# Group A's attention: keys on the partitions, 512 queries in a row, and maxima from products of their own

## The chip, the cores and the metric

One Trainium2 chip; the kernel runs on one of its cores. The engines named below are PE (matrix products; PEld is its weight load), DVE (vector), ACT (scalar, which also evaluates the exponential), POOL (GpSimd) and SP, whose queue issues most of the transfers. The metric is the time of one execution on the device in microseconds (us); the median of three runs is given.

## The reference

The program is one step of a trunk layer with D = 1024 for 2048 latent tokens and 256 context tokens. A combined projection feeds three head groups: A, attention with 6 query heads and 2 key heads of 64; B, a gated DeltaNet in two directions; C, neighbourhood attention. Their outputs are joined by an output projection, and a SwiGLU follows. The change is in group A, where every latent query attends to all 2048 latent and 256 cached keys; context queries attend to the 256 context keys:

```python
def one_block(q_blk):
    sc = jnp.einsum('bqhgd,bkhd->bhgqk', q_blk, k).astype(jnp.float32) * scale
    p = jax.nn.softmax(sc, axis=-1).astype(v.dtype)
    return jnp.einsum('bhgqk,bkhd->bqhgd', p, v)
...
o_a = blocked_attention(qa, jnp.concatenate([ka, ka_ctx.astype(dt)], axis=1),
                        jnp.concatenate([va, va_ctx.astype(dt)], axis=1))
```

Group B solves a small triangular system per chunk of 64 tokens and then runs over the chunks in order (v_new = u - w s; s = s decay + k v_new), both ways.

## The kernel before

Tokens lie in tiles of 128: 16 latent, 2 context, so 18 key tiles with the cached ones. The stages run one after the other: phase_b projects group B, phase_ac projects C and then A and meanwhile prepares the DeltaNet, group_a is the attention, group_c and phase_out follow, then the ffn.

Operands of attention are split into a high and a low part (each exact in the fast product type). KA holds the keys transposed: partitions 0 to 63 the high parts, 64 to 127 the low parts of the same 64 dimensions, for both key heads. k_split makes it: PE transposes a tile of keys in which each dimension stands twice, ACT copies all 128 partitions as the high part, and DVE subtracts that from the second half (split_stack). q_stack does likewise for a tile of 128 queries and gives the high and low part of q, both on all 128 partitions.

group_a before goes through pairs of query tiles (index g, 8 latent and 1 context) and pairs of heads (pr); within these through 2 heads and 2 tiles, which gives 96 latent passes of 128 queries and one head. A pass has

- the scores with queries on the partitions: per 512 keys two products (high q, low q) against KA, in three PSUM tiles Sa and Sb (1024 keys) and Sc (256);
- on DVE the maximum of each (line 1220) and of the three (1224); on ACT the exponentials into P with the maximum as bias and the row sums as a by-product (1228);
- 18 transposes of P by PE (function turn) and their copies into PT by ACT (evac, line 1034), since the product with V needs the keys on the partitions;
- after four passes, the product with V (pv_pieces): 64 columns of weights, 256 queries, both heads into the halves of one PSUM tile po; later a transpose of the result and a multiplication by the reciprocal row sums, and a transfer to oa_d.

turn's and pv_pieces' pieces wait in lists (trs, pvs, late, extra) and are taken out one at a time between the score products, so that PE has work while DVE and ACT are at the maxima and exponentials. The order in which the code is written is the order of PE's instructions; on the others a scheduler places what is written, and what stands under high_priority comes earlier.

Two things run beside the attention. From pass RA = 6 on each pass takes one step of recur, the recurrence over the chunks (PSUM tile rx, tiles rS, rv, rU; its Pool operation rSe; line 971). And bg.run(2.0) lets the solves of the triangular systems go on (lines 843 and 844: a product into stmp and a reduction into sW), up to an estimate of that many us.

The start of A hangs on phase_ac's end: the last k_split writes KA (lines 1022, 1023), v_load brings V, and the first two query tiles have been stacked.

Of the kernel before, what the change touches and what calls it, by code (L numbers as in the profile page):

```python
# [18 lines left out]
NLAT = 16  # L19
NCTX = 2  # L20
NT = 18
# [38 lines left out]
class K:  # L60
# [34 lines left out]
    def setup(self):  # L95
        nc, a = self.nc, self.a
        self.ident = self.ctile("ident", [128, 128])
        nc.sync.dma_start(self.ident, a["ident"])
        self.mhalf = self.ctile("mhalf", [128, 1])
        nc.gpsimd.memset(self.mhalf, -0.5)  # L100

# [290 lines left out]
    def phase_ac(self, es_a, es_p, HB=3):  # L392
# [6 lines left out]
        self.qp = [es_p.enter_context(tc.tile_pool(name="A_q", bufs=2))]  # L399
        self.Q, self.qds = {}, {}  # L400
        es3 = ExitStack()
        bps = es3.enter_context(tc.tile_pool(name="b_ps", bufs=2, space=PSUM))
        with ExitStack() as es:
# [172 lines left out]
            kds = {}  # L576

# [14 lines left out]
            def k_dups(q):  # L592
                KS, KSp = self.KA
                kd = kds.pop(q)
                if q < 4:
                    self.k_split(KS, kd, [(i % 2, 4 * q + i // 2) for i in range(8)], bps)
                elif q == 4:
                    self.k_split(KSp, kd[:, 4:8], [(i % 2, i // 2) for i in range(4)], bps)
                else:
                    self.k_split(KS, kd[:, 0:4], [(i % 2, NLAT + i // 2) for i in range(4)], bps)  # L600

            def after(t):
# [5 lines left out]
                if t in (4, 5):  # L608
                    self.q_load(t - 4, kdp, 2)
                if t in (10, 11):  # L610
                    self.q_stack(t - 10, 0, 4, bps)
                    self.q_stack(t - 10, 4, 6, bps)
# [12 lines left out]
            with tc.high_priority(offset=HP):  # L625
                while pend:
                    a_flush()
            self.need_solves(0)
# [225 lines left out]
    def recur(self, wk, bank):  # L854
# [88 lines left out]
        for n in range(36):  # L943
# [40 lines left out]
            for d in range(2):  # L984
                v.tensor_copy(vn[hf[d], d], pv[hf[d], :256])
# [19 lines left out]
            v.tensor_copy(o, po)  # L1005
# [13 lines left out]
    def split_stack(self, dst, p):  # L1019
# [3 lines left out]
        nc.vector.tensor_tensor(dst[64:128], p[64:128], dst[64:128].bitcast(F32), ALU.subtract)  # L1023
# [22 lines left out]
    def k_split(self, KS, src, dst, pst):  # L1046
# [4 lines left out]
        for i0 in range(0, n, 4):  # L1051
# [5 lines left out]
            for i in range(m):  # L1057
# [6 lines left out]
                self.split_stack(KS[:, h, 128 * j:128 * (j + e - i)], p[:, 128 * i:128 * e])  # L1064

    def q_stack(self, t, h0, h1, pst):

        if h0 == 0:
            self.Q[t] = [self.qp[t // 2 % 2].tile([128, 6, 128], F32R, tag=f"q{n}", name="q", bufs=2) for n in "hl"]
        self.q_split(self.Q[t][0][:, h0:h1], self.Q[t][1][:, h0:h1], self.qds[t][:, h0:h1], h1 - h0, pst)  # L1070

# [16 lines left out]

    def group_a(self):
        nc, tc, a = self.nc, self.tc, self.a  # L1090
        self.EV = ()
        self.oa_d = [self.dtile(f"oa{t}", [128, 384]) for t in range(NT)]
        with ExitStack() as es:
            sp = es.enter_context(tc.tile_pool(name="A_p", bufs=2))
            tp = es.enter_context(tc.tile_pool(name="A_pt", bufs=4))
            wk = es.enter_context(tc.tile_pool(name="A_w", bufs=2))
            self.qp.append(wk)
            psS = es.enter_context(tc.tile_pool(name="A_S", bufs=1, space=PSUM))
            pst = es.enter_context(tc.tile_pool(name="A_t", bufs=2, space=PSUM))
            pso = es.enter_context(tc.tile_pool(name="A_o", bufs=1, space=PSUM))  # L1100
            rec = self.rec = self.recur(self.rwk, lambda: pst.tile([128, 512], F32, tag="pt", name="rx"))
            KS, KSp = self.KA
            V, Vp = self.VA
            groups = [(2 * g, 2 * g + 1) for g in range(NT // 2)]
            OA = {}
            Q = self.Q
            q_load = lambda t: self.q_load(t, wk, 1)
            q_stack = lambda t, h0, h1: self.q_stack(t, h0, h1, pst)

            def pv_pieces(g, pr, PT, rs):  # L1110

                lat = g < 8
                nk = NT if lat else 2
                Vx = V if lat else Vp
                st = {}

                def mm(j0, j1):
                    if j0 == 0:
                        st["po"] = pso.tile([128, 256], F32, tag="po", name="po")
                    for j in range(j0, j1):  # L1120
                        for h2 in range(2):
                            self.pe.matmul(st["po"][64 * h2:64 * h2 + 64, :], lhsT=Vx[:, j, (2 * pr + h2) // 3, :],
# [912 lines left out]
```

## Time and profile before

| | |
|---|---|
| median of 3 runs | 3837.43 us (3836.22 to 3840.2) |
| the profiled execution's own time | 3837.47 us |
| its span in the trace | 3835.5 us |
| granted PE clock, mean | 0.974 |
| first score product of group A to the last latent product with V | 826.7 to 1625 us |

The profile is of one execution. Its page gives busy shares of the engines and 40 slices of the span (95.9 us each); group A's latent part lies in slices 9 to 17:

```profile
PE   8997999969999999989999969999999998899999
PEld 5887988956777777778878869999999998688787
DVE  4784477689655555568765576677667664322433
ACT  4223322236666666657865643343334333322221
POOL 0002322620000000000003355556555553000111
```

Each digit is the busy share in tenths. A group's row reads: line, engine, operation, output <- inputs, shapes, count, then busy us and the mean of one in ns, then how long the engine stood idle ahead of it and for what. A row of the timeline has start, duration and operation. Matrix products overlap their neighbours, so their durations add up to more than the time that they take.

### The profile page before, as it was taken

What the parts mean: (1) busy time and instruction counts of PE and PEld (TensorE: products, weight loads), DVE (VectorE), ACT (ScalarE), POOL (GpSimd) and SP (SyncE); (2) the same over time, 40 slices, a digit from 0 to 9 for tenths busy, and PEclk for the clock granted to TensorE, in tenths of its full rate; (3) what the DMA queues carried; (4) which work ended last, traced back from release to release, by engine and by line L of the source; (5) the groups of instructions that cost most, each with busy time, mean ns of one, the idle gap of its engine ahead of it and who ended that gap; (6) DMA issues with size and microseconds to landing.
All of it is one profiled execution on the core that took longest, in us unless ns stands there. A gap on an engine that the chain in (4) does not pass through costs nothing. (4 is left out here: it accounts for less than half of the span.)

```text
span 3835.5 us, 64839 instructions
## 1 busy us (share of the span) xinstructions
PE 3607.6 (94%) x24526; PEld 3166.5 (83%) x24526; DVE 2308.8 (60%) x4786; ACT 1723.1 (45%) x3552; POOL 966.3 (25%) x1135
## 2 busy tenths in 40 slices
PE   8997999969999999989999969999999998899999
PEld 5887988956777777778878869999999998688787
DVE  4784477689655555568765576677667664322433
ACT  4223322236666666657865643343334333322221
POOL 0002322620000000000003355556555553000111
PEclk9998999989999999999999989999999999899999
DMA  7565877741211112255325643333333332633654
GB/s 270 200 210 175 259 223 225 197 116 48 55 48 51 44 46 52 64 160 144 90 79 186 213 132 99 98 108 108 105 93 97 101 96 75 208 111 125 194 187 133
DMA packets 649081, 501.15 MB, mean 131 GB/s; under 512 B 253681, under 2 KB 577120, under 8 KB 646464
## 3 DMA queue, kind: packets, MB, share of 16 engines
q1 hardware_dynamic: 645984, 493.41, 42.9%
q8 instruction: 193, 3.16, 0.4%
q10 hardware_dynamic: 2624, 3.55, 0.3%
q14 instruction: 120, 0.98, 0.1%
q0 software_dynamic: 160, 0.05, 0.0%
HBM read 348.14 MB, written 148.73 MB: 130 GB/s over the span
## 5 line engine op out<-in xcount | busy, mean ns | idle before, releaser
L37 PE MATMUL pd<-wd,ao 128*128 128x512 f32 x2376 | 550.3, 394 | 26.1 <-DMA wr<-in_w_down_dram 15.0
L37 PEld LDWEIGHTS pd<-wd,ao 128*128 128x128 f32 x2376 | 450.6, 190 | 125.7 <-ACT ao L1695 15.4
L37 PE MATMUL Y<-hop,gop 128*128 128x384 f32 x2376 | 452.3, 338 | 22.4 <-ACT hop L1695 9.8
L1034 ACT ACTIVATE PT<-pt 128x512 f32<-128x512 f32 (+1 forms) x600 | 331.9, 553 | 256.3 <-PE pt L37 249.4
L37 PEld LDWEIGHTS Y<-hop,gop 128*128 128x128 f32 x2376 | 422.1, 191 | 24.2 <-ACT hop L1695 10.1
L1696 DVE TENSOR_TENSOR gop<-S,gop 128x512 fp32r<-128x512 f32 x264 | 235.6, 893 | 167.3 <-ACT gop L1695 157.6
L37 PE MATMUL X<-hop,gop 128*128 128x384 f32 x1584 | 306.2, 342 | 18.7 <-DVE hop L1696 8.9
L37 PE MATMUL po<-PT,V 128*64 128x256 f32 (+1 forms) x3072 | 313.5, 341 | 2.2 <-ACT PT L1034 1.9
L37 PE MATMUL pso<-whi,hi 128*128 128x384 f32 (+2 forms) x864 | 288.8, 334 | 25.3 <-ACT whi L255 13.8
L37 PEld LDWEIGHTS X<-hop,gop 128*128 128x128 f32 x1584 | 283.5, 190 | 20.8 <-DVE hop L1696 9.6
L37 PE MATMUL pt<-ident,P 128*128 128x128 f32 x1752 | 284.9, 280 | 14.9 <-ACT PT L1034 7.9
L37 PE MATMUL Z<-hop,gop 128*128 128x384 f32 x1584 | 297.7, 336 | 0.0
L37 PE MATMUL pso<-whi,lo 128*128 128x384 f32 (+2 forms) x864 | 282.6, 327 | 7.6 <-DMA lo<-hl 7.6
L37 PE MATMUL pso<-wlo,hi 128*128 128x384 f32 (+2 forms) x864 | 282.9, 327 | 0.8 <-DVE wlo L256 0.5
L37 PEld LDWEIGHTS Z<-hop,gop 128*128 128x128 f32 x1584 | 278.7, 189 | 0.1
L37 PEld LDWEIGHTS pt<-ident,P 128*128 128x128 f32 x1752 | 200.3, 141 | 94.4 <-ACT PT L1034 36.3
L1695 ACT ACTIVATE gop<-S 128x512 fp32r<-128x512 f32 x264 | 166.2, 630 | 228.2 <-PE Y L37 124.9
L971 POOL TENSOR_TENSOR rSe<-rS,eh 64x128 f32<-64x128 f32 x144 | 55.0, 400 | 811.6 <-DVE rS L1003 780.9
L1696 DVE TENSOR_TENSOR gop<-wr,gop 128x512 fp32r<-128x512 f32 x198 | 200.9, 1015 | 83.8 <-ACT gop L1695 77.6
L37 PEld LDWEIGHTS po<-PT,V 128*64 128x64 f32 x3072 | 180.4, 136 | 79.3 <-issue 33.7
L1695 ACT ACTIVATE gop<-wr 128x512 fp32r<-128x512 f32 x198 | 125.2, 632 | 245.3 <-PE Z L37 174.7
L1696 DVE TENSOR_TENSOR ao<-ar,ao 128x1408 fp32r<-128x1408 f32 x72 | 127.4, 1769 | 145.1 <-ACT ao L1695 143.1
(323 smaller groups left out, 7208.1 us busy)
## 6 DMA issues: line engine op xcount, KB each, us to landing
ar<-a SPq DMA_DIRECT2D x72, 704.0 KB, 4.8
wr<-in_w_gu_dram SPq DMA_DIRECT2D x66, 512.0 KB, 4.1
wr<-in_w_gu_dram SPq DMA_DIRECT2D x132, 256.0 KB, 3.4
a<-o SPq DMA_DIRECT2D x396, 64.0 KB, 2.1
wm<-in_w_mod_dram SPq DMA_DIRECT2D x48, 512.0 KB, 4.1
hi<-hh SPq DMA_DIRECT2D x36, 512.0 KB, 5.4
lo<-hl SPq DMA_DIRECT2D x36, 512.0 KB, 6.4
st<-ptk SPq DMA_DIRECT2D x18, 768.0 KB, 4.1
```

The costliest lines, as they stand in the source:

```text
L37: r = f(*x, **kw)
L971: nc.gpsimd.tensor_tensor(Se[hh[x], d], S[hh[x], d, :, hh[x]], e.unsqueeze(2).to_broadcast([64, 2, 64]), ALU.mult)
L1034: self.nc.scalar.activation(out, p, AF.Copy)
L1695: self.nc.scalar.activation(hi, raw, AF.Copy)
L1696: self.nc.vector.tensor_tensor(lo, raw, hi.bitcast(F32), ALU.subtract)
```

## The change

Group A goes through 15 units instead: 4 latent blocks of 512 queries and the context block of 256, each with 3 pairs of heads (p with p + 3, so one head of either key head). Per unit and key tile j:

- scores with the keys on the partitions: for each of the two heads two products of 512 queries into one PSUM tile ST: KA against the high part of q (QH), and K1 against QL. K1 holds the keys' high part on 64 partitions and a row of ones as the 65th; QL holds the low part of q and, in its 65th row, minus the query's maximum. So ACT takes the exponential without a bias.
- P then already has the keys on the partitions, so the product with V uses it as it is (512 queries per product); the transposes of P and their copies are gone.
- the row sums, now sums over partitions, are collected: Pool adds most P tiles up (accp), DVE every sixth (accd); at the unit's end a product with ones sums over the partitions, and transposes bring sums and output to queries on the partitions.
- the maxima come from products of their own, of high parts alone, with queries on the partitions (SM; max_steps): 40 per unit (4 query tiles, 2 heads, 5 pieces of up to 512 keys), each reduced by DVE. They are made during the unit before. Four small products turn the maxima of one head into a row, which ACT copies into QL.

The first unit's maxima are written into the last sweep of the projections (mid) and, for the last piece of the latent keys, to the start of A. There too K1 is filled: a copy of KA's high half per key head from SBUF to SBUF by SP's queue and a fill with ones by DVE. For that, k_split puts the high part of key head 1 on partitions 64 to 127 (flip). The queries of the first block are loaded and stacked ahead of A, four tiles instead of two. In recur two copies out of PSUM move from DVE to ACT; the transfer of the output moves from ACT's queue to SP's. bg.run gets 0.9 per key tile and recur 0.45 of a step.

The core of the diff:

```diff
+            psM = es.enter_context(tc.tile_pool(name="A_M0", bufs=2, space=PSUM))
+            self.mg0 = self.max_steps(0, 0, self.mx0, psM, (4, 0, 1, 2))
...
             def mid(t0, j, i):
                 if t0 == NT - HB:
                     with tc.high_priority(offset=HP):
                         for f, q in MID.get((j, i), ()):
                             f(q)
+                        for _ in range(4):
+                            next(self.mg0, None)
...
-                v.tensor_copy(vn[hf[d], d], pv[hf[d], :256])
+                nc.scalar.activation(vn[hf[d], d], pv[hf[d], :256], AF.Copy)
...
-            v.tensor_copy(o, po)
+            nc.scalar.activation(o, po, AF.Copy)
...
+    def max_steps(self, b, p, mx, psM, chunks):
+        ks, nk, nq = (self.KA[0], 2304, 512) if b < 4 else (self.KA[1], 256, 256)
+        for c in chunks:
+            w = min(512, nk - 512 * c)
+            for qi in range(nq // 128):
+                for x in range(2):
+                    S = psM.tile([128, 512], F32, tag="SM", name="SM")
+                    self.pe.matmul(S[:, :w], lhsT=self.QB[b][0][:, p + 3 * x, 128 * qi:128 * qi + 128],
+                                   rhs=ks[:, x, 512 * c:512 * c + w], start=True, stop=True)
+                    with self.tc.high_priority(offset=1000):
+                        self.nc.vector.tensor_reduce(mx[:, qi, x, c:c + 1], S[:, :w], AX.X, ALU.max)
+                    yield
...
+            for x, y in zip(self.K1, self.KA):
+                nc.vector.tensor_copy(x[64:65].rearrange("p h k -> p (h k)"),
+                                      self.one[64:65, 0:1].to_broadcast([1, 2 * x.shape[2]]))
+                for h in range(2):
+                    nc.sync.dma_start(x[0:64, h].bitcast(F32), y[64 * h:64 * h + 64, h].bitcast(F32))
+            psS = es.enter_context(tc.tile_pool(name="A_S", bufs=3, space=PSUM))
+            psM = es.enter_context(tc.tile_pool(name="A_M", bufs=2, space=PSUM))
+            pso = es.enter_context(tc.tile_pool(name="A_o", bufs=1, space=PSUM))
...
+            def maxes(b, p, at=None):
...
+                yield from self.max_steps(b, p, mx, psM, (3,) if at else range(nch))
...
+                with tc.high_priority(offset=1000):
+                    nc.vector.tensor_reduce(mn[:, :n], mx[:, :n, :, :nch], AX.X, ALU.max, negate=True)
+                QL = self.QB[b][1]
+                for x in range(2):
+                    t = pst.tile([128, 512], F32, tag="pt", name="mrow")
+                    for qi in range(n):
+                        self.pe.matmul(t[64:65, 128 * qi:128 * qi + 128], lhsT=mn[:, qi, x:x + 1], rhs=self.ident,
+                                       start=True, stop=True, skip_group_check=True)
+                    with tc.high_priority(offset=1000):
+                        nc.scalar.activation(QL[64:65, p + 3 * x, :nq], t[64:65, :nq], AF.Copy)
+                    yield
...
+            def scores(b, p, j):
...
+                P = sp.tile([128, 2, 512], F32, tag="P", name="P")
...
+                for x in range(2):
+                    S = psS.tile([128, 512], F32, tag="S", name="ST")
...
+                    self.pe.matmul(S[:, :nq], lhsT=ks[:, x, kc], rhs=QH[:, h, :nq], start=True, stop=False)
+                    self.pe.matmul(S[:, :nq], lhsT=k1[0:65, x, kc], rhs=QL[0:65, h, :nq], start=False, stop=True)
+                    nc.scalar.activation(P[:, x, :nq], S[:, :nq], AF.Exp)
+                return P
...
+                for x in range(2):
+                    self.pe.matmul(po[64 * x:64 * x + 64, :nq], lhsT=V[:, j, x, :], rhs=P[:, x, :nq], start=(j == 0),
+                                   stop=(j == nk - 1), skip_group_check=True)
+                if j % 2 == 0:
+                    next(mg, None)
...
+                if j % 6 == 5:
+                    ad = accs[1][:, :, :nq]
+                    if j == 5:
+                        nc.vector.tensor_copy(ad, w)
+                    else:
+                        nc.vector.tensor_tensor(ad, ad, w, ALU.add)
+                elif j == 1:
+                    nc.gpsimd.tensor_tensor(accs[0][:, :, :nq], P0[:, :, :nq], w, ALU.add)
+                elif j:
+                    nc.gpsimd.tensor_tensor(accs[0][:, :, :nq], accs[0][:, :, :nq], w, ALU.add)
...
+                if j == nk - 1:
+                    due += finish(b, p, po, accs)
+                if i >= 12 and b < 4:
+                    credit += 0.45
+                    if credit >= 1:
+                        credit -= 1
+                        next(rec, None)
+                self.bg.run(0.9)
```

How the instructions stand in a row follows for the places on which most hangs. PE, in the middle of the latent part before (Sa, Sb, Sc are scores, pt transposes, po the product with V, rx the recurrence):

```order
L37 MATMUL Sa<-KA_6616,q 128x512 x4
L37 MATMUL pt<-ident,P 128x128 x4
L37 MATMUL Sb<-KA_6616,q 128x512 x4
L37 MATMUL pt<-ident,P 128x128 x4
L37 MATMUL Sc<-KA_6616,q 128x256 x2
L37 MATMUL pt<-ident,P 128x128 x4
L37 MATMUL po<-PT,V 64x256 x6
```

and in the changed kernel (ST scores, SM the products for the maxima):

```order
L37 MATMUL ST<-QH,KA_6618 128x512
L37 MATMUL ST<-QL,K_9138 128x512
L37 MATMUL ST<-QH,KA_6618 128x512
L37 MATMUL ST<-QL,K_9138 128x512
L37 MATMUL SM<-KA_6618,QH 128x512
L37 MATMUL pt<-ident,qd 128x128 x2
L37 MATMUL po<-P,V 64x512 x2
L37 MATMUL SM<-KA_6618,QH 128x512
```

The four transposes between the score products are gone; a key tile's four score products and one SM stand between two bursts of po, now at 512 columns, and the K1 products are new.

DVE, while the solves run, before (mx the maxima, stmp and sW the solve):

```order
L1220 TENSOR_REDUCE mx<-Sa 128x1
L843 TENSOR_TENSOR stmp<-sW 128x1
L1240 TENSOR_REDUCE sm<-sm 128x1
L1220 TENSOR_REDUCE mx<-Sb 128x1
L1220 TENSOR_REDUCE mx<-Sc 128x1
L844 TENSOR_REDUCE sW<-stmp 128x1
L1241 RECIPROCAL rs<-sm 128x1
```

and in the second unit of the changed kernel:

```order
L1124 TENSOR_REDUCE mx<-SM 128x1
L854 TENSOR_REDUCE sW<-stmp 128x7
L853 TENSOR_TENSOR stmp<-sW 128x128
L853 TENSOR_TENSOR stmp<-sW 128x64
L854 TENSOR_REDUCE sW<-stmp 128x8
L1124 TENSOR_REDUCE mx<-SM 128x1
L854 TENSOR_REDUCE sW<-stmp 128x8
L853 TENSOR_TENSOR stmp<-sW 128x136
```

Three reductions of up to 1024 keys per pass became single ones of 512, one here and there between the solve's pairs.

DVE at the start of A, before:

```order
L847 COPY sC<-sW 128x1024
L1023 TENSOR_TENSOR KA_6616<-pt,KA_6616 64x512 x2
L1023 TENSOR_TENSOR KA_6617<-pt,KA_6617 64x256 x2
L1220 TENSOR_REDUCE mx<-Sa 128x1
L1220 TENSOR_REDUCE mx<-Sb 128x1
```

and now (one is the fill of K1's row of ones, mx_6623 the first unit's maxima):

```order
L853 TENSOR_TENSOR stmp<-sW 128x136
L853 TENSOR_TENSOR stmp<-sW 128x72
L854 TENSOR_REDUCE sW<-stmp 128x8 x2
L853 TENSOR_TENSOR stmp<-sW 128x1
L1142 CAST K_9138<-one 1x4608
L1124 TENSOR_REDUCE mx_6623<-SM 128x1 x8
L854 TENSOR_REDUCE sW<-stmp 128x1
L853 TENSOR_TENSOR stmp<-sW 128x208
L1168 TENSOR_REDUCE mn<-mx_6623 128x8
```

Between the keys' last split and the first minimum there are now solve pairs, the fill and eight maxima.

POOL, during A, before:

```order
L971 TENSOR_TENSOR rSe<-rS_9521,eh 64x128 x4
L971 TENSOR_TENSOR rSe<-rS_9522,eh 64x128 x4
L971 TENSOR_TENSOR rSe<-rS_9521,eh 64x128 x4
L971 TENSOR_TENSOR rSe<-rS_9522,eh 64x128 x4
```

and now:

```order
L1305 TENSOR_TENSOR accp<-P 128x1024
L1307 TENSOR_TENSOR accp<-accp,P 128x1024 x9
L981 TENSOR_TENSOR rSe<-rS_9640,eh 64x128 x4
L1307 TENSOR_TENSOR accp<-accp,P 128x1024 x4
L1305 TENSOR_TENSOR accp<-P 128x1024
L1307 TENSOR_TENSOR accp<-accp,P 128x1024 x6
L981 TENSOR_TENSOR rSe<-rS_9641,eh 64x128 x4
L1307 TENSOR_TENSOR accp<-accp,P 128x1024 x6
```

The recurrence's short operations now stand in one row with 14 additions per unit.

More of the change, by code (lines that the diff above doesn't have):

```diff
@@ L100, in setup @@
         nc.gpsimd.memset(self.mhalf, -0.5)
+        self.one = self.ctile("one", [128, 32])
+        nc.gpsimd.memset(self.one, 1.0)
     def mod_setup(self, sb, ps):
@@ L627, in phase_ac @@
                     a_flush()
+                for _ in self.mg0:
+                    pass
             self.need_solves(0)
@@ new lines, in group_a @@
+            self.K1 = [k1.tile([65, 2, n], F32R, name=f"K1{i}") for i, n in enumerate((2304, 256))]
+            for x, y in zip(self.K1, self.KA):
[4 more added lines that the diff above has]
+            psS = es.enter_context(tc.tile_pool(name="A_S", bufs=3, space=PSUM))
@@ L1148, in turn @@
-            def turn(P, PTh, nk, qi):
-                def piece(k0):
-                    m = min(4, nk - k0)
-                    p = pst.tile([128, 512], F32, tag="pt", name="pt")
-                    for j in range(m):
-                        self.pe.transpose(p[:, 128 * j:128 * j + 128],
-                                          P[:, 128 * (k0 + j):128 * (k0 + j) + 128], self.ident)
-                    self.evac(0, PTh[:, k0:k0 + m, 128 * qi:128 * qi + 128],
-                              p[:, :128 * m].rearrange("p (j t) -> p j t", j=m))
-                return [lambda k0=k0: piece(k0) for k0 in range(0, nk, 4)]
@@ L1249, in group_a, with keys @@
-            self.k_split(KSp, kx.rearrange("p h t r d -> p (h t) r d"), [(0, 0), (0, 1), (1, 0), (1, 1)], pst)
-            drain()
+            blocks = [range(4 * b, 4 * b + 4) for b in range(4)] + [range(NLAT, NT)]
+            units = [(b, p) for b in range(5) for p in range(3)]
+            def keys(b):
+                i = 0 if b < 4 else 1
+                return self.KA[i], self.K1[i], self.VA[i], (NT, 2)[i], (512, 256)[i]
+            def maxes(b, p, at=None):
+                nq = keys(b)[4]
+                n, nch = nq // 128, (keys(b)[3] + 3) // 4
+                mx = at or wk.tile([128, 4, 2, 5], F32, tag="mx", name="mx")
+                yield from self.max_steps(b, p, mx, psM, (3,) if at else range(nch))
+                mn = wk.tile([128, 4, 2], F32, tag="mn", name="mn")
+                with tc.high_priority(offset=1000):
[9 more added lines that the diff above has]
+                    yield
@@ L1252, in group_c @@
+            for q in (due, extra):
+                while q:
+                    q.pop(0)()
+            self.k_split(KSp, kx[0].rearrange("p h t r d -> p (h t) r d"), [(0, 0), (0, 1), (1, 0), (1, 1)], pst)
     def group_c(self):
```

273 lines of the change are left out of this document (130 added, 143 removed).

## Prediction

> **What bounds the kernel now.** I read the page's busy lines, then the stretches in time, then the groups of instructions inside group A.
>
> ```profile
> PE 3607.6 (94%) x24526; PEld 3166.5 (83%) x24526; DVE 2308.8 (60%) x4786; ACT 1723.1 (45%) x3552; POOL 966.3 (25%) x1135
> ```
>
> ```profile
> core 0: us, PE busy (x) PEld busy (x) DVE busy (x) ACT busy (x) POOL busy (x), PEclk, DMA share, GB/s
> 827.00:1625.00 798.00, 775.75 (x7438) 588.46 (x7437) 499.87 (x1248) 537.14 (x1111) 47.69 (x124) 1.00 0.22 55
> 860.00:900.00 40.00, 38.05 (x312) 26.28 (x312) 38.41 (x131) 28.93 (x61) 0.00 (x0) 1.00 0.22 53
> 900.00:1000.00 100.00, 95.67 (x936) 72.49 (x932) 87.67 (x274) 65.31 (x136) 6.33 (x16) 1.00 0.21 50
> 1000.00:1100.00 100.00, 98.69 (x968) 75.32 (x968) 56.43 (x123) 68.57 (x141) 6.04 (x16) 1.00 0.20 55
> 820.00:830.00 10.00, 4.44 (x12) 3.39 (x13) 6.22 (x14) 0.77 (x2) 3.49 (x12) 0.50 0.76 179
> ```
>
> The latent part of group A takes 798 us, 66.5 per twelfth (one of the new units), and PE is busy in 97% of it. Until about 980 us DVE is nearly as full (38.41 of 40 us), since the background solves run there; afterwards it has 44 us in 100 free. Pool does nearly nothing.
>
> ```profile
> L37 PE MATMUL pt<-ident,P 128*128 128x128 f32 x1728 | 279.9, 280 | 10.2 <-ACT PT L1034 7.7 <-DVE q L1028 1.9 <-DVE ro L1005 0.2
> L1034 ACT ACTIVATE PT<-pt 128x512 f32<-128x512 f32 x384 | 228.8, 596 | 174.0 <-PE pt L37 167.4
> L37 PE MATMUL po<-PT,V 128*64 128x256 f32 x1728 | 227.3, 390 | 0.0
> ```
>
> These are what the change aims at: 1728 transposes of P (144 per unit) and their evacuation. A mean of a pipelined product is longer than its place in the row, so I price PE by starts:
>
> ```profile
> 999.96 1.52 PE L37 MATMUL po<-PT,V 128*64 128x256 f32 x12
> 1001.40 0.65 PE L37 MATMUL pt<-ident,P 128*128 128x128 f32 x4
> 1001.99 1.08 PE L37 MATMUL po<-PT,V 128*64 128x256 f32 x8
> 1002.90 0.66 PE L37 MATMUL rx<-rS,rsT 128*64 128x128 f32 x8
> ...
> 1005.52 0.60 PE L37 MATMUL pt<-ident,P 128*128 128x128 f32 x4
> 1005.87 1.18 PE L37 MATMUL Sb<-KA,q 128*128 128x512 f32 x4
> 1006.89 0.60 PE L37 MATMUL pt<-ident,P 128*128 128x128 f32 x4
> ...
> 2060.09 0.39 PE L37 MATMUL m<-WH,hi 128*128 128x512 f32 x1
> 2060.32 0.39 PE L37 MATMUL m<-WL,hi 128*128 128x512 f32 x1
> sum 600.00, PE 104.33 PEld 98.71 DVE 87.89; mean PE 17.39 PEld 16.45 DVE 14.65
> ```
>
> A 512-column product of this kind costs 0.23 us from start to start. Four transposes and four such products fill 1005.52 to 1006.89, 1.37, so a transpose costs 0.11. Eight PV records followed by another 64-column product take 0.91, 0.11 each. Twelve followed by 128-column work take 1.44 for 1.32, and the four transposes ahead of a PV burst 0.59 for 0.44: going to 64 columns and back costs some 0.30 a burst. The last line is the instructions on the tile of the recurrence (rx) in six stretches of 100 us: 73 steps, 1.43 us of PE and 1.2 of DVE a step.
>
> **PE after the change.** Per key tile: four products of 0.227 (0.91), PV at 512 columns for two heads, four records of twice 0.1075 (0.86), one switch (0.30): 2.07, times 18 is 37.2. Maxima: 32 products of 0.227 and 8 of half that, 8.2. The row that carries minus the maximum, the ones-products, the output's and sums' transposes and their switches: an estimate of 5.7 by the same rows. Recurrence, 8.1 steps of 1.43 less shared switches: 10.4. Together 61.5 against 66.5 before. Unit 0 has hardly any recurrence (51), unit 11 no maxima to make (53). Twelve units: 51 + 10 x 61.5 + 53 = 719, so **-79 us if PE alone sets the pace**. The transposes that go free only this, because 40 maxima products, the shorter PV bursts and one switch per key tile come back.
>
> **DVE and Pool.** What was one exp with its row sum now leaves a sum over partitions: 14 Pool additions of 128x1024 per unit and 3 DVE operations. The maxima become 40 DVE reductions per unit.
>
> ```profile
> 830.47 1.22 DVE L1220 TENSOR_REDUCE mx<-Sb 128x1 f32<-128x1024 f32 x1 [0.48 <-PE Sb L37]
> 831.61 0.41 DVE L1220 TENSOR_REDUCE mx<-Sc 128x1 f32<-128x256 f32 x1
> 826.00:860.00 34.00, 12.10 (x65) 0.87 0.67 163
> 860.00:900.00 40.00, 22.21 (x89) 1.00 0.22 53
> 900.00:1000.00 100.00, 33.76 (x152) 1.00 0.21 50
> 1000.00:1100.00 100.00, 0.00 (x0) 1.00 0.20 55
> ```
>
> 1024 elements step in 1.14, 256 in 0.33: 512 in 0.60, so 40 maxima are 21.8 us a unit. The last four rows are the solve's instructions on tile stmp alone: 306, half additions or products and half reductions, in 68 us: 0.445 a pair. In the written order of the changed kernel 32, 74 and 69 pairs fall into units 0, 1 and 2, none after. Unit 1 on DVE: 21.8 + 33.0 solve + 3.5 sums (three of 1.15) + 6.3 recurrence (8.1 steps of 1.2, less two copies of some 0.2 that go to ACT) + 6 for q, outputs and reciprocals = 71; unit 2: 67; unit 0: 43. PE gives 51, 61.5 and 61.5, 174 together. The maxima buffers are two, so a late reduction stops PE's next maximum product and all behind it: in units 1 and 2 DVE sets the pace, +15 for nothing but its busy time.
>
> **The lock.** No row of group A has a long Pool operation beside a DVE operation of two SBUF inputs. The nearest stand in the ffn:
>
> ```profile
> 2344.46 0.69 DVE L1696 TENSOR_TENSOR gop<-S,gop 128x512 fp32r<-128x512 f32 x1 [1.35 <-ACT gop L1695]
> 2346.10 1.02 DVE L1696 TENSOR_TENSOR gop<-S,gop 128x512 fp32r<-128x512 f32 x1
> 2348.18 1.61 DVE L1696 TENSOR_TENSOR gop<-wr,gop 128x512 fp32r<-128x512 f32 x1
> 2345.28 1.29 POOL L1786 TENSOR_TENSOR S<-wr 128x512 f32<-128x512 f32 x1 [3.28 <-DVE gop L1696]
> 2347.96 1.29 POOL L1787 TENSOR_TENSOR S<-S,wr 128x512 f32<-128x512 f32 x1
> L1832 POOL TENSOR_TENSOR o<-u,u x66: 992/1466/1742, 2281.6 to 3252.1; 128x384 f32<-128x384 f32 x66
> L1786 POOL TENSOR_TENSOR S<-wr x66: 1262/1290/1868, 2227.2 to 3205.8; 128x512 f32<-128x512 f32 x66
> ```
>
> Alone the DVE operation takes 0.69. Where Pool runs it ends 0.55 after Pool's end, both times (2347.12 after 2346.57, 2349.79 after 2349.25): it waits for Pool nearly to its end. The Trainium skill has this as a rule ("SBUF — State Buffer", section "Who interferes with whom"): DVE's second port pair is shared with GpSimd, and whichever holds it shuts the other out for the whole instruction, reductions excepted; by it the sum would be the one below, and by the solve rows above, which are no longer beside Pool's 16 short operations than without (0.222 against 0.250 us), 59 us less. Those Pool operations fill only 6% of that stretch, so I go by the ffn rows.
>
> Pool's price: 992 ns for 384 and 1262 for 512 elements at the least, 2.1 ns an element, 2.34 us for 1024; 14 are 33 us a unit, so Pool itself keeps up. Each holds some 2.2 us. A solve product comes every 0.9 us in units 1 and 2, so one that meets Pool loses about 1.5 us (1.2 in unit 0, where they are fewer): 14 x 1.5 = 21, 17 in unit 0. Between 0 (by the solve rows) and 14 x 2.2 = 31 I take these. Units 0 to 2: 60 + 92 + 88 = 240, **+66** over PE's 174, at most +100, at least +15.
>
> **Later units.** DVE needs about 38 of 61.5 us and Pool 37. Three additions on DVE per unit still meet Pool, and maxima queue behind them while PE has two buffers: up to 5.5 us a unit, 2 taken, times nine **+18** (0 to 50).
>
> **Start.** The new key copy K1 can go only after the last write of the keys.
>
> ```profile
> 826.68 2.05 PE L37 MATMUL Sa<-KA,q 128*128 128x512 f32 x4 [1.91 <-DVE KA L1023]
> ar<-a SPq DMA_DIRECT2D x72, 704.0 KB, 4.8
> ```
>
> PE's first product of A waited for DVE's key split until 826.68. DVE gets 32 maxima (19 us) and a fill of 4608 elements (some 5 by 1.14 per 1024) into the tail of the projections, beside the solves; with 6.22 of 10 us busy there about half finds room: 12 late. Then the copy, two of 590 KB, 5 to 7 us by the 704 KB row. On SP's queue the next q loads and the recurrence's loads stand behind it. Unit 0's last 8 maxima, the minimum, the product that turns it into a row and ACT's copy into QL: about 5. First scores near 850, **+24** (10 to 35). The context units and group C: nothing, they start from whatever A ends at; their two copies moved to ACT per step lie beside PE work.
>
> **Sum.** -79 + 66 + 18 + 24 = +29. Against the profiled run's 3837.47 (span 3835.5, 2 us around it; the median shown is 3837.43) that is **3866 us**, 3846 to 3900 for this case. A measurement of this kernel tells a change from none at about 0.2%, 7.7 us.
>
> **Rivals.**
> - A, faster: the solve operations hardly lose to Pool (the stmp rows), and DVE only costs its busy time: -79 + 15 + 10 + 24 = -30, 3807. It decides if units 0 to 2 together take less than 203 us. For it: stmp operations are short, so many may fit between Pool's; against: Pool has 33 us of additions a unit and issues back to back once behind. 0.27.
> - B, half the lock: +37 in place of +66, 3837, no change. 0.12.
> - C: the 65-row product pays the switch that 64 columns pay; no row has one. 36 x 0.30 = 10.8 a unit in the nine units that PE paces: +97, 3963. 0.06.
> - D: Pool adds at the rate of its slow rows (1868 ns for 512, 3.7 an element, 3.9 us): Pool then fills 59 of 61.5 us, and a meeting costs DVE 2.9 instead of 1.5, 42 times: +59, 3925. 0.09.
> - The main case: 0.46.
>
> The range, 3785 to 3945, takes in A to 22 below its value, B, the main case and D to 20 above, and leaves out C and the tails, under 2 in 10. Faster is A (0.27), within 0.2% B (0.12), slower the rest (0.61).
>
> **What would show it.** In the profile after: first ST near 850 and first PV soon after; starts of ST 0.23 apart, and a key tile with no recurrence and no stall near 2.5 us; units 0 to 2 with PE visibly below 90% and its maxima products waiting for DVE's mx; solve operations that end 0.3 to 0.5 us after a Pool addition; units 3 to 11 near 61 to 64 us with PE above 95%; Pool additions near 2.3 us. I am wrong if stmp operations keep their 0.3 us beside Pool (A), if the ST pair with K1 takes over 0.6 us (C), if Pool's additions are near 3.9 us (D), or if ACT, which now has 36 exps, the copies of the recurrence and the q splits, holds PE up in the later units.

## The result and the profile after

The changed kernel takes 3885.47 us (median of 4 runs, 3880.37 to 3889.75) against 3838.81 for the kernel before on the same chip: a ratio of 1.0121, 95% interval 1.0103 to 1.0139, 46.7 us slower. The profiled execution took 3880.37 us with a span of 3878.3, 42.8 more than before. Half of it has arisen when group A's latent part begins, some 20 us later than before. The other half arises within it: from the first exponential of a unit to the next unit's, the twelve units take 66.0, 104.1, 89.4, then 63.0, 64.4, 63.1, 62.3, 64.7, 63.3, 63.1, 62.6 and 52.8 us (66.5 each before), 819 for 798. From the end of the latent part on the trace is as long as before (2211 us).

From the page after, the busy line and the slices of the PE clock:

```profile
PE 3612.4 (93%) x22684; PEld 3023.8 (78%) x22684; DVE 2355.1 (61%) x4611; ACT 1498.2 (39%) x3045; POOL 1369.8 (35%) x1307
...
PEclk9998999987899999999999979999999999899999
```

The clock's row of the page before:

```profile
PEclk9998999989999999999999989999999999899999
```

PE is busy no less than before (3612 for 3608 us), ACT 225 us less, POOL 403 more. The granted clock is lower than before in the tenth and eleventh slice (7 and 8 for 9 and 9), from 873 to 1067 us, where units 0 to 2 are. The stretches of units 0, 1, 2, then 3 to 10 (columns as in the prediction's table):

```profile
848.00:914.00 66.00, 57.12 (x242) 28.72 (x241) 59.59 (x121) 22.79 (x42) 35.05 (x18) 0.90 0.36 82
914.00:1018.00 104.00, 77.50 (x493) 43.88 (x492) 88.40 (x222) 26.38 (x50) 36.51 (x22) 0.80 0.17 40
1018.00:1108.00 90.00, 70.25 (x500) 39.81 (x498) 77.81 (x192) 25.39 (x49) 39.73 (x24) 0.89 0.11 27
1108.00:1614.00 506.00, 505.02 (x3859) 295.23 (x3859) 294.29 (x543) 205.24 (x404) 298.38 (x200) 1.00 0.19 52
```

From unit 3 to 10 PE is busy all the time at full clock: 506 us for eight units, 63.3 each, 3.2 less than before. In units 0 to 2 PE is idle for 55 of 260 us, and DVE is the fuller engine. What PE waited for most there (sum, times, longest):

```profile
PE SM L37 <- DVE mx L1124: 17.1, 20, 2.0
PE pt L37 <- DVE rsy L944: 7.4, 1, 7.4
PE pt L37 <- ACT rv L995: 6.8, 1, 6.8
PE rx L37 <- DVE rS L1013: 6.5, 1, 6.5
PE rx L37 <- ACT rv L995: 6.4, 1, 6.4
```

Two kinds: many short waits for the maxima, and a few of 4 to 7 us for single operations of the recurrence (rsy, rv, rS). The longest one ended when DVE had come to the copies into rsy, which stand between pairs of the solve:

```profile
931.91 0.28 DVE L944 COPY rsy<-rx 32x128 f32<-32x128 f32 x1
932.31 0.68 DVE L853 TENSOR_TENSOR stmp<-sW 128x168 f32<-128x168 f32 x2
933.54 0.30 DVE L944 COPY rsy<-rx 32x128 f32<-32x128 f32 x1
933.99 1.08 PE L37 MATMUL pt<-ident,oT 128*128 128x128 f32 x4 [7.40 <-DVE rsy L944]
```

The lock itself, DVE against POOL on the timeline:

```profile
926.60 2.40 DVE L853 TENSOR_TENSOR stmp<-sW 128x152 f32<-128x152 f32 x2
926.16 2.35 POOL L1307 TENSOR_TENSOR accp<-accp,P 128x1024 f32<-128x1024 f32 x1 [1.14 <-ACT P L1190]
```

Two solve products that otherwise take some 0.6 us together last 2.40 here, until just after POOL's addition ends (929.00 and 928.51). Of 166 solve products in units 0 to 2, the 128 that overlap no POOL operation take 0.305 us in the mean, the 38 that do 1.52; 32 of the 38 overlap an addition, the others a short operation of the recurrence. POOL's additions are as priced:

```profile
L1307 POOL TENSOR_TENSOR accp<-accp,P x156: 2338/2370/3232, 857.6 to 1664.7; 128x1024 f32<-128x1024 f32 x156
```

And a key tile of the later units, start to start:

```profile
1328.79 0.50 PE L37 MATMUL SM<-KA,QH 128*128 128x512 f32 x1
1329.12 0.40 PE L37 MATMUL ST<-QH,KA 128*128 128x512 f32 x1
1329.36 0.40 PE L37 MATMUL ST<-QL,K 65*128 65x512 f32 x1
1329.60 0.40 PE L37 MATMUL ST<-QH,KA 128*128 128x512 f32 x1
1329.83 0.40 PE L37 MATMUL ST<-QL,K 65*128 65x512 f32 x1
1330.07 0.40 PE L37 MATMUL SM<-KA,QH 128*128 128x512 f32 x1
1330.40 1.08 PE L37 MATMUL po<-P,V 128*64 128x512 f32 x4
1331.41 0.49 PE L37 MATMUL SM<-KA,QH 128*128 128x512 f32 x1
```

2.62 us, with two products for maxima; the 65-row products stand at the same 0.23 as the others.

### The profile page after: what moved, and what is told of

It reads as the page before. It is cut to its first block, busy times and chain, and to the rows that moved or that the text cites. A ratio compares the mean times of both kernels' runs of the same rounds, so it can differ in the third digit from the quotient of the medians.

```text
span 3878.3 us, 60982 instructions
## 1 busy us (share of the span) xinstructions
PE 3612.4 (93%) x22684; PEld 3023.8 (78%) x22684; DVE 2355.1 (61%) x4611; ACT 1498.2 (39%) x3045; POOL 1369.8 (35%) x1307
## 4 chain that ended last, share of the span: by engine, by line
PE 63%; DVE 7%; DMA 3%; ACT 2%; issue 2%; POOL 1%; SPq 0%; ACTq 0%; POOLq 0%; DVEq 0%
PE pd L37 13%; PE Y L37 10%; PE Z L37 7%; PE po L37 7%; PE X L37 7%; PE ST L37 5%; PE rx L37 4%; PE SM L37 3%; PE pt L37 3%; PE m L37 2%; PE S L37 2%; DVE stmp L853 2%; DVE mx L1124 1%; DMA y<-oa 1%; PE mrow L37 1%
## 5 line engine op out<-in xcount | busy, mean ns | idle before, releaser
L1307 POOL TENSOR_TENSOR accp<-accp,P 128x1024 f32<-128x1024 f32 x156 | 371.0, 2378 | 226.5 <-ACT P L1190 223.3
L1190 ACT ACTIVATE P<-ST 128x512 f32<-128x512 f32 (+1 forms) x444 | 240.2, 589 | 424.2 <-PE ST L37 421.1
L1124 DVE TENSOR_REDUCE mx<-SM 128x1 f32<-128x512 f32 (+1 forms) x492 | 303.7, 629 | 136.7 <-PE SM L37 128.9
L37 PE MATMUL SM<-KA,QH 128*128 128x512 f32 (+1 forms) x492 | 208.3, 442 | 37.1 <-DVE mx L1124 36.2
L37 PEld LDWEIGHTS SM<-KA,QH 128*128 128x128 f32 x492 | 92.0, 194 | 190.7 <-DVE mx L1124 129.8
L37 PE MATMUL po<-P,V 128*64 128x512 f32 x864 | 240.6, 636 | 0.0
```

Source lines behind the costliest of these rows:

```text
L37: r = f(*x, **kw)
L1124: self.nc.vector.tensor_reduce(mx[:, qi, x, c:c + 1], S[:, :w], AX.X, ALU.max)
L1190: nc.scalar.activation(P[:, x, :nq], S[:, :nq], AF.Exp)
L1307: nc.gpsimd.tensor_tensor(accs[0][:, :, :nq], accs[0][:, :, :nq], w, ALU.add)
```

## The experiments

Unless said otherwise, each is the changed kernel with the edit shown. Times are compared with the kernel before on the same chip; the lengths of units are those of the profiled execution, from first exponential to first exponential.

**No additions on POOL in units 0 to 2.**

```diff
-                elif j:
+                elif j and u > 2:
                     nc.gpsimd.tensor_tensor(accs[0][:, :, :nq], accs[0][:, :, :nq], w, ALU.add)
```

> Leaves out Pool's additions of P in the first three units but for each unit's first one (the row sums of these units are incomplete). The changed kernel takes 66 + 104 + 89 = 259.5 us for units 0 to 2; 38 solve products that overlap a Pool addition last 1.52 us there, the 128 others 0.305. Lock theory: all solve products fall to about 0.31, DVE gets some 46 us back, units 0 to 2 take 195 to 215 us. Rival (order): PE stands because the recurrence's DVE operations are queued behind solve pairs, whatever Pool does; then units 0 to 2 stay above 240. The scheduler moves some 50 solve pairs from units 1 and 2 into units 3 and 4 when the additions are gone, so units 0 to 4 are compared too: 387 us in the changed kernel, by the lock theory 320 to 340.

Measured (one run): 3843.55 us against 3833.42, 10 us slower instead of 47. Units 0 to 2 take 58.1, 89.1 and 77.5, 224.7 for 259.5; units 3 to 11 are unchanged, and no solve is left for them. The instructions on stmp in units 0 to 2, changed kernel and then this one:

```profile
848.00:1108.00 260.00, 121.16 (x336) 0.86 0.20 46
```

```profile
848.00:1073.00 225.00, 82.94 (x336) 0.89 0.23 54
```

The same 336 instructions take 38 us less, and the units 35 us less: DVE's lost time comes back nearly one to one. So the lock costs 35 us (each unit's first addition, which stays, not counted), and neither expectation holds whole, since 224.7 is still 36 more than the prediction had for PE's and DVE's work alone (189). That POOL held PE up by keeping P's buffers, another way to read this run, is not borne out: PE's list of waits in the changed kernel has none for POOL. The schedule of the solves that I read as moved to units 3 and 4 was, in time, where it had been.

**The solve spread over eight units.**

```diff
-                self.bg.run(0.9)
+                self.bg.run(0.3)
...
-                v.tensor_tensor(tv, M[:n, c0:c1, c0:i], ...)
+                self.dv.tensor_tensor(tv, M[:n, c0:c1, c0:i], ...)
```

Here self.dv keeps the written order of what is issued through it; DVE's additions of P go through it too.

> The background gets 0.3 in place of 0.9 per key tile, and solve products keep their written order against DVE's additions, so that 33, 57, 10, 20, 17, 16, 13, 10 solve pairs fall into units 0 to 7 in place of 33, 74, 69. If it is DVE's load in the first units that costs (with its waits for Pool): unit 0 unchanged at 66, unit 1 about 92, unit 2 about 66, units 3 to 7 1 to 3 us longer each, 30 us less in all, about 3853. If the additions cost the same wherever a solve product meets them, because the operations behind hold PE up in any unit: the loss moves into units 2 to 7, and the time stays within 10 us.

Measured: 3880.48 us, ratio 1.0115 (1.0098 to 1.0132): no gain. Units 1 and 2 fall to 84.1 and 66.1, but units 3 to 7 take 75.6, 68.0, 74.2, 71.2 and 67.6, 39 us more than before the edit. Of the solve products now 77 overlap a POOL operation, at 1.49 us each (38 before); 74 of them overlap an addition (32 before). So spread over more additions, more of them meet one, and the maxima behind them stop PE in any unit: PE waits 21.7 us for maxima in units 3 to 7, where it had next to no waits before. Part of the result is the edit's own: in unit 1 PE waits 14.4 us at once for one of DVE's additions, which now has to keep its place in the written order.

**The recurrence only from unit 3 on.**

```diff
-                if i >= 12 and b < 4:
-                    credit += 0.45
+                if i >= 54 and b < 4:
+                    credit += 0.57
```

> The recurrence starts at unit 3 instead of late in unit 0, with 0.57 of a step per key tile, so that as many steps lie in the latent part. Rival (order): the waits of PE for the recurrence's DVE and ACT operations in units 0 to 2 (41 us in the trace) vanish, units 0 to 2 take about 215, units 3 to 11 get 2.1 more steps of 1.43, 3 us each: some 20 us less in all. Lock and DVE load alone: DVE has 18 steps of 0.8 less in units 0 to 2, which take about 240, and the later units take back 25: no gain.

Measured (one run): 3878.51 against 3833.42. Units 0 to 2 take 67.9, 73.7 and 63.9, 205.5 in all, lower than either theory said; but some 54 solve products slip into unit 3, which takes 89.2, and units 4 to 11 pay 23 us for the steps moved there. Two units here have 54 solve products each beside the same additions: unit 1 without the recurrence takes 73.7 us, with DVE busy for 69.9; unit 3 with it takes 89.2, with DVE busy for 68.8 and PE for 72.5. Beside solves alone DVE is nearly full; with both, neither engine is, so that time goes in which one waits for the other. That agrees with a cost of the recurrence beside the solve that is not the lock's. The run by itself does not size it: unit 3 also has some 10 steps of PE's work that unit 1 has not, and units 1 and 2 have fewer solve products than in the changed kernel (54 and 27 for 72 and 60).

**Row sums from a 65th column of V.**

```diff
-                    self.pe.matmul(po[64 * x:64 * x + 64, :nq], lhsT=V[:, j, x, :], rhs=P[:, x, :nq], ...)
+                    self.pe.matmul(po[x][0:65, :nq], lhsT=V[:, j, x, :], rhs=P[:, x, :nq], ...)
...
-                    nc.gpsimd.tensor_tensor(accs[0][:, :, :nq], accs[0][:, :, :nq], w, ALU.add)
```

> The row sums come from a 65th column of ones in V: the two heads' products with V go to two PSUM tiles of 65 rows, and the additions on Pool and DVE, the ones-products and the transposes of the sums are gone; the score tiles have two PSUM buffers instead of three. Lock theory: with no addition on Pool the solve products take 0.31, DVE's load alone is left in units 0 to 2 (about 200 us for 259.5), the later units save 2 to 3 us: about 3800. Rivals: a product with 65 columns costs more than with 64 or pays another switch (over 0.1 us each, 36 a unit: 4 us a unit more, 3840), or two score buffers stop PE in each key tile (units 3 to 11 above 66).

Measured: 3914.99 us, ratio 1.0208 (1.0192 to 1.0223), the slowest. Units 0 to 2 take 70.2, 74.6 and 72.3, with no rise left over the later ones (71.4 to 73.4): with no addition on POOL those units have become like the others. That says less about the lock than the first run, since PE's own work has become longer and hides DVE's, and the solve lies elsewhere (84, 69 and 14 of its products in units 0 to 2, for 34, 72 and 60): PE waits only 7.5 us in the whole latent part. Each later unit costs 9 us more. PE's timeline there:

```profile
1405.50 1.88 PE L37 MATMUL po<-P,V 128*65 128x512 f32 x4
1406.81 0.68 PE L37 MATMUL SM<-KA,QH 128*128 128x256 f32 x1
1407.42 0.67 PE L37 MATMUL rx<-rS,rsT 128*64 128x128 f32 x8
```

The four records take 1.31 until the next product starts, and that one then 0.61 instead of its 0.13 or so: near 1.75 in all. One by one they start 0.43 us apart, four times the 0.11 that a transpose of 128 takes. In the changed kernel, where the four took 1.01, the records of the two 64-column halves start 7 ns apart and the second pair 0.48 after the first. So the two halves run side by side, and the products with 65 columns do not: the first rival, and larger than I had written it.

**The recurrence's operations ahead of the solve's.**

```diff
-                        next(rec, None)
+                        with tc.high_priority(offset=1000):
+                            next(rec, None)
```

> The changed kernel with the recurrence's steps written under high priority, so that their DVE operations stand ahead of the solve's in DVE's order; Pool's additions as they were. Order theory: PE's waits for these operations in units 0 to 2 (41 us) go, units 0 to 2 take about 220 instead of 259.5, the whole about 3845. Load theory (DVE has the same work, the solve pairs pushed back meet Pool and PE's maxima a little later, in units 1 to 3): less than 12 us gained over units 0 to 3 (322.5 in the changed kernel).

Measured: 3879.15 us, ratio 1.0114 (1.0099 to 1.0129). Units 0 to 3 take 88.7, 82.1, 73.4 and 77.1. The waits for rsy, rv and rS are gone from PE's list; of 36 us at steps of the recurrence two of 4.7 before its products (rx) are left, while the waits for maxima in units 1 to 3 go from 9 to 17. Units 1 to 3 are 24 us shorter; unit 0 gives 23 us back:

```profile
PE ST L37 <- DMA K<-KA: 16.2, 1, 16.2
```

The recurrence's loads went ahead too, and the second copy K1 stood behind them on SP's queue (issued at 861.06, the first at 837.58). While PE stood for it, DVE went on with the solve: 50 of its products lie in unit 0 (34 in the changed kernel), 117 in units 1 to 3 (132). Over units 0 to 3 the time is 321.3 us for 322.5, the number of the load theory. So the run shows that the order makes these waits, and not what they cost in time. A version with these copies put first:

```diff
                 for h in range(2):
-                    nc.sync.dma_start(x[0:64, h].bitcast(F32), y[64 * h:64 * h + 64, h].bitcast(F32))
+                    with tc.high_priority(offset=4000):
+                        nc.sync.dma_start(x[0:64, h].bitcast(F32), y[64 * h:64 * h + 64, h].bitcast(F32))
```

> The kernel with the recurrence's steps under high priority again, with the copies K1 ahead of the recurrence's loads on SP's queue. There PE waited 16 us for the second copy. If that was the queue's order: unit 0 about 70 instead of 88.7, the whole about 3863, and the 24 us that the order in units 1 to 3 gave are seen in the time. If the copy is slow for another reason (the loads beside it): unchanged at 3879.

Measured: 3893.48 us, ratio 1.0140 (1.0124 to 1.0155): the wait for K1 is gone, and the next thing on the queue is late, the loads of the second block's queries:

```profile
PE pt L37 <- DMA qd<-qa: 22.5, 1, 22.5
```

Unit 0 takes 95.7 with 58 solve products, and units 1 to 3 are 25 us shorter than in the changed kernel, with 109. (The profiled execution, 3882.69 us, was the fastest of the four.) A queue's order without a late load in unit 0 was not found, so what the recurrence's order costs by itself stays open: the 24 and 25 us in units 1 to 3 are in part solve work that moved into unit 0.

**Row sums by PE in units 0 to 2** (with the recurrence under high priority, K1's copies where they were).

```diff
+                if ps:
+                    for x in range(2):
+                        self.pe.matmul(sq[32 * x:32 * x + 32, :nq], lhsT=self.one, rhs=P[:, x, :nq], start=(j == 0),
+                                       stop=(j == nk - 1), skip_group_check=True)
-                if j % 6 == 5:
+                elif j % 6 == 5:
```

> As the last one, and in units 0 to 2 the row sums are made by PE: per key tile and head a product of P with 32 columns of ones, added up in a PSUM tile, in place of the additions on Pool and DVE (the score tiles then have two PSUM buffers). Without Pool's lock and without the order DVE's busy time is left, 43, 71 and 67, less 3.5 each for the sums, and PE's 51, 61.5 and 61.5 with 0.5 a key tile more: units 0 to 2 take about 205, the whole about 3830. Rival: 32 columns cost as much as the 65 did (0.33 a record, 1.3 a key tile): PE alone then needs 85 in units 1 and 2, and the three take about 240.

Measured: 3864.55 us, ratio 1.0072 (1.0057 to 1.0087). Units 0 to 2: 85.1, 80.6, 79.7. The stretches of the three units and PE's one long wait there:

```profile
846.00:931.00 85.00, 69.31 (x309) 29.68 (x308) 65.94 (x222) 22.57 (x42) 1.94 (x4) 0.88 0.29 63
931.00:1012.00 81.00, 80.79 (x559) 39.01 (x557) 65.99 (x206) 25.82 (x51) 3.02 (x8) 1.00 0.19 48
1012.00:1092.00 80.00, 80.00 (x564) 38.58 (x563) 41.21 (x93) 24.98 (x49) 3.54 (x10) 1.00 0.13 30
```

```profile
PE ST L37 <- DMA K<-KA: 15.7, 1, 15.7
```

But for the late K1 there is no wait left (0.2 us for maxima), and in units 1 and 2 the clock is 1.00: with neither the lock nor the order, they take PE's work. As with the 65th column, that work is longer here than in the changed kernel, and 86, 66 and 14 solve products lie in units 0 to 2, so the run does not price the lock and the order. Its sum product is dear:

```profile
894.41 1.05 PE L37 MATMUL sq<-P,one 128*32 128x512 f32 x4
895.40 0.50 PE L37 MATMUL SM<-KA,QH 128*128 128x512 f32 x1
```

0.99 a key tile, 18 a unit: 61.5 + 18 = 79.5, which is what units 1 and 2 take. The expectation had 0.5 a tile; the rival's three units, about 240, came nearer (245.4, 16 of them the late K1).

**Products with V of two key tiles in one burst.**

```diff
-                for x in range(2):
-                    self.pe.matmul(po[...], lhsT=V[:, j, x, :], rhs=P[:, x, :nq], ...)
+                for jj, Pj in ((j - 1, P0), (j, P)) if j % 2 else ():
+                    for x in range(2):
+                        self.pe.matmul(po[...], lhsT=V[:, jj, x, :], rhs=Pj[:, x, :nq], ...)
```

> The products with V of two key tiles in one burst (six buffers for P, one each for the sums). If a burst's way to 64 columns and back costs PE 0.30, units 3 to 11 take 9 x 0.30 = 2.7 us less each, about 60.5 for 63, some 24 us in all there. If the switch is hidden, or P now waits for Pool: no change or more.

Measured: 3893.48 us, ratio 1.0151 (1.0136 to 1.0166). Units 3 to 10 take 63.1, 64.4, 66.2, 60.9, 64.0, 67.4, 63.9 and 63.3, 513 for 506. The burst does cost less:

```profile
1326.11 1.94 PE L37 MATMUL po<-P,V 128*64 128x512 f32 x8
1327.97 0.50 PE L37 MATMUL SM<-KA,QH 128*128 128x512 f32 x1
```

1.86 for two key tiles instead of 2.02, and unit 11, which has hardly any maxima to make, takes 51.2 for 52.8. But in the other units the maxima products now come two at a time, and PE waits 17 us for their reductions from unit 3 on (0.8 in the changed kernel). The saving went into that wait and, in units 0 to 2 (261.7), into nothing.

**All maxima of the first unit at A's start.**

```diff
-                        for _ in range(4):
-                            next(self.mg0, None)
...
-            for _ in maxes(0, 0, self.mx0):
+            for _ in maxes(0, 0):
```

> All 40 maxima of the first unit at the start of A, none beside the last projections. The last projection product ends at 831.7 in the changed kernel and at 813.4 in the one before; if the maxima there are what delays it, the projections end near 815, then 40 products and reductions at 0.64 take 26 us, the copy K1 is done meanwhile, and the first scores stand near 850 as before: within 6 us. If they were free beside the projections, the first scores come 15 to 20 us later, at 862 to 867.

Measured: 3878.18 us, ratio 1.0114 (1.0097 to 1.0130). The last projection product ends at 807.7, against 831.7 with the maxima beside it and 813.4 in the kernel before, so it is the maxima that delay the projections. Yet the first scores come at 855.75 instead of 846.97, 9 us later and between the two cases expected, and units 0 to 2 take 249.9 instead of 259.5: nothing in sum. What was saved goes into the maxima: at A's start PE and DVE alternate at 0.79 us a maximum (two products per 1.58):

```profile
823.20 1.40 PE L37 MATMUL SM<-KA,QH 128*128 128x512 f32 x2 [0.18 <-DVE mx L1120]
824.78 1.40 PE L37 MATMUL SM<-KA,QH 128*128 128x512 f32 x2 [0.18 <-DVE mx L1120]
```

**The solve's products on POOL.**

```diff
-                v.tensor_tensor(tv, M[:n, c0:c1, c0:i], ...)
+                (nc.gpsimd if self.solved > 2 else v).tensor_tensor(tv, M[:n, c0:c1, c0:i], ...)
```

> The products of the last two solves (152 of the 175 pairs in group A) go to Pool; the reductions stay on DVE. Pool's operations cannot overlap each other, so no solve product meets an addition, and DVE sheds 152 x 0.305 = 46 us of work and the 38 us it lost. Lock theory: units 0 to 2 take about 200 us for 259.5 and the whole about 3825, unless Pool, with 33 us of additions and some 25 to 40 of products a unit, each waiting for a reduction, becomes the one that holds P's buffers: then PE stands for P and the three units take 230 or more.

Measured: 3858.29 us, ratio 1.0054 (1.0039 to 1.0069), 27 us better than the changed kernel against its own comparison. Units 0 to 2: 67.9, 82.4, 83.6. DVE falls to 54.8 us in unit 1 and POOL rises to 67.7 of 82: 234 in sum, which is the second case's number, but not by its reason. PE's list has no wait for P. It has 22 us for maxima, and the solve's reductions on DVE, with maxima behind them in the order, wait 36 us for POOL's products in units 1 and 2.

```profile
914.00:996.00 82.00, 67.61 (x492) 38.69 (x492) 54.80 (x140) 25.66 (x50) 67.67 (x87) 0.94 0.19 46
```

The same with the recurrence under high priority and K1 first:

> The last one, with the recurrence's steps under high priority and the copies K1 ahead of the recurrence's loads on SP's queue. If what is left in units 1 and 2 is the recurrence behind the solve on DVE: 10 to 20 us less than the last one in units 0 to 2. If Pool is the bound: the same as the last one.

Measured: 3872.30 us, ratio 1.0092 (1.0075 to 1.0109). Units 1 and 2 gain 12.5 us (76.4, 77.1), with 88 solve products for 134; unit 0 loses 28 (96.2) to the same late query loads, 22.5 us. And the solve's products on POOL as in the first of these two, with half of POOL's additions in units 0 to 2 given to PE:

```diff
+                elif sq is not None and j and j % 2 == 0:
+                    for x in range(2):
+                        self.pe.matmul(sq[32 * x:32 * x + 32, :nq], lhsT=self.one, rhs=P[:, x, :nq], start=(j == 2), ...)
```

> The products of the last two solves on Pool, as in e9_pool_solve, and in units 0 to 2 every second P tile summed by PE's products with ones (1.0 us a tile, 8 a unit), so that Pool has 6 additions a unit there instead of 14. If Pool's work in those units is what holds PE (69.7 us busy of 82 in unit 1): Pool falls to about 46 and units 0 to 2 go to PE's work, about 60 + 70 + 70 = 200 us for 234, the whole about 3825, just under the kernel before. If it is the recurrence behind DVE's solve that is left: PE's 8 us come on top of 82 and 84, and the time stays at 3855 or more.

Measured: 3857.87 us, ratio 1.0050 (1.0036 to 1.0064), as without it: units 0 to 2 take 74.6, 92.8 and 74.3. By the operations that start in each unit POOL is down from 42, 70 and 69 us to 35, 55 and 28, and PE still waits 14.2 us for maxima, 9.5 for the minimum after them and 4.0 for the recurrence. The forecast 200 us of the POOL case did not come. But the solve's products lie elsewhere too, 84 in unit 1 and 20 in unit 2 where they were 65 and 69, and this run does not tell that apart from POOL's load. None of these versions beats the kernel before.

## Why the prediction was right

It said 3866 us, 3846 to 3900 for its main case, and slower; measured 3885. The main case holds: PE saves in the later units, and units 0 to 2 and the start cost more than that. Two of its four terms came near their size for another reason than the one given, which is luck, and one was too small. Against the profiled execution:

- **PE's own work** was -79 in sum. Units 3 to 10 take 63.3 each where the prediction had 61.5 and 2 of waits, unit 11 52.8 for 53, and in the run with PE's sums units 1 and 2 came out near the model's 79.5. The price of 0.23 for the 65-row product and 2.37 for POOL's addition (2.34 forecast) rule out the rivals of a dear K1 product and of slow additions.
- **Start**: 847 for 850, +20 for +24, but by another chain than I gave, so the size was luck. The fill took 2.55 us, not 5; what the maxima cost was the projections' end, 18 us later; and the copy of the keys took 10.4 us to land, not 5 to 7, at about 846, beside the row of maxima:

```profile
834.89 11.98 SPq L1145 DMA_DIRECT2D K<-KA  x4
841.77 3.58 PE L37 MATMUL mrow<-ident,mn 128*1 128x128 f32 x16 [1.51 <-DVE mn L1168]
846.97 0.76 PE L37 MATMUL ST<-QH,KA 128*128 128x512 f32 x1 [1.63 <-DVE sW L854]
```

- **Later units**: the 18 us for waits were about right in size (559 for 545 in nine units, 14) and wrong in kind. PE's list shows only 0.8 us of waits in units 3 to 10, so the difference is PE's own: a key tile of 2.62 for 2.53.
- **Units 0 to 2** are the step that was mis-sized: +66 forecast, +85 measured (259.5 for 174), and its inner split was off by more. DVE did not set the pace as the sum had it: it is busy for 226 us where the sum filled 240, and idle for 34 of the 260. In parts:
  - The lock had 51 of the 66 in the forecast and is 35. DVE loses 38 us where the sum gave 59: 32 solve products meet the 42 additions, not one for each. DVE's busy time had the other 15.
  - The sum did not have the order on DVE: PE's 4 to 7 us waits for the recurrence's few DVE operations, which stand behind solve pairs. In the run without additions PE waits 30 us in units 0 to 2, 26 of them at steps of the recurrence or for their results. What these waits would give back if they went, no run shows.
  - Nor did it have the clock. In that run PE is busy 195 of 225 us for work worth 174, at a clock of 0.85 to 0.91. By an estimate that takes PE's speed to follow the clock (products start 0.42 us apart at 0.50, 0.23 at 1.00), busy time times granted clock, unit by unit (54.65 at 0.91, 72.29 at 0.85, 68.44 at 0.91), its work is worth 173 us at full clock, the model's 174; so the 21 us more go with the clock. The same estimate from the rows of the changed kernel above gives 176: there the 85 us are 55 in which PE stood and some 29 that the lower clock adds.
- **Rival A** (DVE hardly loses to POOL) is refuted by 1.52 against 0.305, and by 259.5 us for units 0 to 2 where it had less than 203. **Rival B** (half the lock) was nearer for the lock alone, but the total came out above the main case because of the order and the clock.

The rule of the Trainium skill ("SBUF — State Buffer", section "Who interferes with whom") on DVE's shared port pair agrees with the rows of this case: products of two SBUF inputs wait to POOL's end, and a reduction does not, here one in the midst of an addition, 0.69 us as the others:

```profile
1181.54 0.69 DVE L1124 TENSOR_REDUCE mx<-SM 128x1 f32<-128x512 f32 x1 [0.65 <-PE SM L37]
1180.64 2.38 POOL L1307 TENSOR_TENSOR accp<-accp,P 128x1024 f32<-128x1024 f32 x1
```

## What to carry to other kernels

A change that frees the busiest engine for 3 us in 66 still has to pass through the stretch where another engine is full: look at the stage's first units apart, with their own background work, before spreading a gain over all. Long POOL additions beside a stream of short two-input DVE products cost DVE about half an addition at each meeting here, and spreading the products over more time made more of them meet, not fewer. And before moving a step's priority, list what its loads pass on the shared queue: each time that the recurrence's loads went ahead here, the next load behind them came 16 to 22 us late, and the first unit lost about what the later ones gained, or more.

## What the runs showed of the hardware

When PE stands for some microseconds its granted clock falls, and it stays low while work comes in bits; two stretches of the changed kernel, and the whole unit 1 at 0.80:

```profile
930.00:940.00 10.00, 3.72 (x9) 1.30 (x9) 8.56 (x37) 0.00 (x0) 0.00 (x0) 0.50 0.00 0
940.00:950.00 10.00, 8.05 (x55) 5.06 (x55) 9.20 (x31) 1.79 (x3) 2.35 (x1) 0.50 0.09 15
```

After a wait of 7.4 us, which ended at 933.99, the clock is 0.50 for 20 us, though PE is 80% busy in the second half. Each long wait is paid again in slower products, which start 0.42 apart there and 0.23 apart at full clock:

```profile
944.88 0.63 PE L37 MATMUL ST<-QH,KA 128*128 128x512 f32 x1
945.30 0.63 PE L37 MATMUL ST<-QL,K 65*128 65x512 f32 x1
```

In the Trainium skill ("TensorE: Matmul & The Clock Gate", part "The HAM clock gate") half rate follows an idle window of about 3.4 us and full rate returns after as long a busy one. The half rate here agrees; the full rate returned later, at 949.9, after 8 us in which PE had no gap (from 941.95 on).

Two products of 64 columns into the two halves of a PSUM tile run side by side: their records start 7 ns apart, four records of 512 take 1.01 us, against near 1.75 with 65 columns, where they start 0.43 apart. The products with 32 columns, on two quarters, took 0.99, no less than 64 columns on two halves.
